# Decoder trunk on one core: hh and hl level with the weights modulo 512 bytes, a norm's rows loaded later, another order of the conformer's output chunks

## Chip, core and metric

One core of a Trainium2 chip runs the whole program. The metric is the device time of one execution in microseconds; the number quoted for a kernel is the median of its runs.

## What is computed

Two layers on x of shape (1, 256, 1024) in float32. Layer 0 mixes with causal block attention and a Mamba-2 scan side by side, layer 1 with a conformer convolution module. Behind every mixer and every feed-forward stands a norm of the residual sum:

```python
for layer in range(2):
    mixed = moba_ssd_mixer(x, ...) if layer == 0 else conformer_conv_module(x, ...)
    x = layer_norm(DN_ALPHA * x + mixed, ln_mix_g[layer], ln_mix_b[layer])
    x = layer_norm(DN_ALPHA * x + swiglu_ffn(x, ...), ln_ffn_g[layer], ln_ffn_b[layer])

def swiglu_ffn(x, w_gate, w_up, w_down):          # 1024 -> 2816 -> 1024
    return (silu(x @ w_gate) * (x @ w_up)) @ w_down

def conformer_conv_module(x, ...):
    val, gate = split(x @ w_pw1 + b_pw1)
    h = causal_depthwise_conv(val * sigmoid(gate), dw_w, dw_b)   # width 31
    return silu(layer_norm(h)) @ w_pw2 + b_pw2
```

## The kernel before

**Weights.** All weights come as 94 chunks of 1 MB, 128 partitions x 2048 numbers, in the order in which they are used. `Flow` streams them: SyncE loads a chunk into wr (three buffers, L445), ScalarE copies each half of it rounded to float32r into wh (L464), and VectorE writes the rest wr - wh into wl (L465). wh and wl have five buffers each. A chunk's place in that ring comes free with `flow.free()`, behind its last matmul.

**Matmuls.** A product of float32 numbers is made of three float32r matmuls: high by high, low by high, high by low (`mm3`, L538 to L540). x itself lies transposed in xhl, high and low parts side by side, so that a gate or up projection needs two matmuls for each block (`wstat2`): the stationary wh against 512 columns of xhl (L715), and wl against the 256 high ones (L716). The result h of a feed-forward's column block j is split into hh and hl (L821, L822). `xstat_out` takes the down projection for two blocks at a time: 24 matmuls with hh or hl stationary and 512 columns of weights moving. The program's names for the outputs are f (gate and up), fh (the first blocks, `by_halves`), fa (down), op (the mixer's output projection, with mh and ml stationary), p (the conformer's), end (the last quarter of the second feed-forward, 256 wide).

**A norm** (`boundary`) works in token halves t and column halves f. `tail(t, f)` does the last chunks' matmuls into one quarter, `sum` adds the residual and takes statistics, `center` and `fin` finish, `flip` transposes x for the next stage. The rows of gain and offset lie in gb, one buffer of 1 MB, broadcast over the partitions by `ln_rows`; the load waits until the norm before has read the buffer. The conformer's output projection has four chunks, the mixer's and the feed-forwards' tails have two.

**The conformer's taps** (`taps`): part of the depthwise convolution runs on TensorE as small matmuls pc against hs, shifted copies that come back through DRAM (hd, then hs), before a transpose ct. The bias of the output projection is put into its four PSUM banks by one matmul each (L1383).

**Order.** The code records all instructions. `issue_order` then simulates the engines with modelled costs and writes an order for each engine: at each step the ready instruction with the longest tail of work behind it, within a patience, SyncE's loads not over 400 matmuls ahead. Within an engine (SyncE's queue too) instructions run in that order, and one that waits holds all behind it.

**Places in SBUF.** Pools lie one behind the other, so an unused tile at the start of one moves all behind it. Where tiles begin in a partition of the built programs, in bytes modulo 512:

| tiles | before | after |
|---|---|---|
| xhl (x, in pool cp) | 128 | 128 |
| wr, wh, wl (pool wp) | 288 | 224 |
| mh, ml of the mixer | 288 | 224 |
| hh, hl of the first feed-forward | 416 | 224 |
| hh, hl of the second | 352 | 224 |

All slices that the matmuls take begin a multiple of 512 bytes further on.

Of the kernel before, what the change touches and what calls it, by code (L numbers as in the profile page):

```python
# [10 lines left out]
F32 = mybir.dt.float32  # L11
# [6 lines left out]
P = 128  # L18
# [4 lines left out]
NJ = HID // P  # L23
# [69 lines left out]
def issue_order(tc, nc, pools):  # L93
# [6 lines left out]
    ins = [i for i in trace if str(i.opcode) not in fixed]  # L100
# [64 lines left out]
    eng = [i.engine for i in ins]  # L165
# [94 lines left out]
    for k in range(N):  # L260
        for j in deps[k]:
            succ[j].append(k)
    dur = [max(c, d * 4 / 360.0) if eng[k] == SP else c for k, (c, d) in enumerate(zip(cst, dma_n))]

# [244 lines left out]
def trunk(ctx: ExitStack, tc: tile.TileContext, pools, w, prm, rows, x, xw, out):  # L509
# [4 lines left out]

    ctx.enter_context(pools.pool(name="gap0", bufs=1)).tile([P, 24], F32, name="gap0")
    wp = ctx.enter_context(pools.pool(name="wp", bufs=1))
    ctx.enter_context(pools.pool(name="gap1", bufs=1)).tile([P, 8], F32, name="gap1")
    pacc = ctx.enter_context(pools.pool(name="pacc", bufs=4, space=PSUM))
# [111 lines left out]
    def boundary(n, tail, acc, gb, head):  # L630
# [10 lines left out]
        for f in range(2):  # L641
            nm.center(0, f)
        tail(1, 0)
        for f in range(2):
            nm.fin(0, f, head is None)
        if head is None:
# [21 lines left out]
            return  # L668
        tail(1, 1, range(tail.n - 1))
        lo0 = nm.flip(0, 0)  # L670
# [114 lines left out]
    class Ffn:  # L785
# [37 lines left out]

        def run(self, last=False):

            nd = NJ // 2
            acc = None
            for j in range(NX, NJ):
                o = wstat2(f"f{self.n}_{j}")
                flow.add(self.side(j, o))  # L830
                if j % 2 == 1 and j < NJ - 1:
                    d = (j - 3) // 2
                    if acc is None:
                        acc = acc4(f"fa{self.n}")
                    xstat_out(acc, [self.h[2 * d + i] for i in range(2)], d == 0,
                              last and j == NJ - 3)
# [3 lines left out]
                                     for d in (nd - 2, nd - 1)])  # L840
            return acc, tail

# [394 lines left out]
    def to_ffn0():  # L1237
# [3 lines left out]
        dg["p"] = dgp.tile([P, 4 * sum(QUADS)], F32, name="dp")  # L1241
        return scope("f0")

    def scope(name):
        st = ExitStack()
        return st, st.enter_context(pools.pool(name=name, bufs=1))

# [17 lines left out]
    flow.add(diagonals(), 70)  # L1265
    gb = ln_rows(1)
    acc, tail = f0.run()

# [181 lines left out]
    def to_ffn1():  # L1450
        cv.st.close()
        return scope("f1")

    f1 = Ffn(1)
    boundary(2, tail, acc, gb, lambda m: f1.head(to_ffn1(), m))
    gb = ln_rows(3)
    acc, tail = f1.run(True)
    boundary(3, tail, acc, gb, None)
# [108 lines left out]
```

## Time and profile before

| | |
|---|---|
| median of 3 runs | 611.28 us (610.76 to 611.39) |
| the profiled execution | 612.4 us |
| its span, first to last instruction | 610.7 us |
| granted TensorE clock, mean of the span | 0.997 of full speed |
| busy: TensorE, VectorE, ScalarE, GpSimd | 595.2, 429.8, 348.0, 63.3 us |
| moved by DMA | 112.37 MB, mean 184 GB/s |

The times are of one profiled execution. PE is TensorE's matmuls, PEld its loads of stationary operands, DVE is VectorE, ACT ScalarE, POOL GpSimd, SPq the DMA issues of SyncE. In a timeline the first number is the start, the second the duration in us; matmuls that follow each other overlap, so the distance of their starts is the pace. Names carry no buffer numbers in the profile.

### The profile page before, as it was taken

What the parts mean: (1) busy time and instruction counts of PE and PEld (TensorE: products, weight loads), DVE (VectorE), ACT (ScalarE), POOL (GpSimd) and SP (SyncE); (2) the same over time, 40 slices, a digit from 0 to 9 for tenths busy, and PEclk for the clock granted to TensorE, in tenths of its full rate; (3) what the DMA queues carried; (4) which work ended last, traced back from release to release, by engine and by line L of the source; (5) the groups of instructions that cost most, each with busy time, mean ns of one, the idle gap of its engine ahead of it and who ended that gap; (6) DMA issues with size and microseconds to landing.
All of it is one profiled execution on the core that took longest, in us unless ns stands there. A gap on an engine that the chain in (4) does not pass through costs nothing.

```text
span 610.7 us, 9423 instructions
## 1 busy us (share of the span) xinstructions
PE 595.2 (97%) x3662; PEld 506.1 (83%) x3662; DVE 429.8 (70%) x723; ACT 348.0 (57%) x613; POOL 63.3 (10%) x98
## 2 busy tenths in 40 slices
PE   8999999999999999999999999899899999999995
PEld 7989898778888888888879885787788888888884
DVE  5788876698596556656697897889756556655636
ACT  5867977447455545554647862565645545555521
POOL 2100020000260000000013941200000000000002
PEclk9999999999999999999999999999999999999998
DMA  8857345428445645555516954726855554554101
GB/s 286 313 242 276 138 151 195 139 77 333 165 188 208 205 162 187 204 175 175 202 70 235 232 152 94 273 86 231 320 203 197 208 190 165 196 201 165 49 0 70
DMA packets 22497, 112.37 MB, mean 184 GB/s; under 512 B 2866, under 2 KB 8242, under 8 KB 10164
## 3 DMA queue, kind: packets, MB, share of 16 engines
q1 hardware_dynamic: 22452, 111.77, 52.3%
q8 instruction: 29, 0.48, 0.3%
q14 instruction: 16, 0.13, 0.1%
HBM read 109.59 MB, written 2.17 MB: 183 GB/s over the span
## 4 chain that ended last, share of the span: by engine, by line
PE 84%; DVE 6%; DMA 3%; ACT 3%; issue 1%; POOL 1%; SPq 0%; DVEq 0%; ACTq 0%; POOLq 0%
PE f L715 23%; PE f L716 12%; PE fa L538 6%; PE fa L540 6%; PE fa L539 6%; PE fh L738 3%; DVE wl L465 2%; PE pc L1356 2%; DMA wr<-in_w_dram 1%; PE op L540 1%; PE p L539 1%; PE p L540 1%; PE p L538 1%; PE op L538 1%; PE op L539 1%
## 5 line engine op out<-in xcount | busy, mean ns | idle before, releaser
L465 DVE TENSOR_TENSOR wl<-wr,wh 128x1024 fp32r<-128x1024 f32 (+1 forms) x188 | 228.5, 1232 | 51.5 <-ACT wh L464 49.0
L464 ACT ACTIVATE wh<-wr 128x1024 fp32r<-128x1024 f32 (+1 forms) x188 | 191.7, 1045 | 78.3 <-issue 43.4
L715 PE MATMUL f<-xhl,wh 128*128 128x512 f32 x640 | 225.4, 394 | 1.5 <-DVE hl L809 1.5
L716 PE MATMUL f<-xhl,wl 128*128 128x256 f32 x640 | 178.5, 279 | 0.0
L715 PEld LDWEIGHTS f<-xhl,wh 128*128 128x128 f32 x640 | 120.0, 187 | 30.4 <-DVE hl L809 1.9
L716 PEld LDWEIGHTS f<-xhl,wl 128*128 128x128 f32 x640 | 120.0, 188 | 1.0
L538 PE MATMUL fa<-wh,hh 128*128 128x512 f32 x172 | 68.0, 395 | 0.0
L539 PE MATMUL fa<-wl,hh 128*128 128x512 f32 x172 | 67.8, 394 | 0.0
L540 PE MATMUL fa<-wh,hl 128*128 128x512 f32 x172 | 67.8, 395 | 0.0
L816 DVE TENSOR_TENSOR h<-f,h 128x256 f32<-128x256 f32 x40 | 17.0, 424 | 70.6 <-ACT h L815 70.6
L573 POOL TENSOR_TENSOR rd<-rs,mhalf 128x1 f32<-128x1 f32 x8 | 4.4, 548 | 377.6 <-DVE rs L570 377.6
L815 ACT ACTIVATE h<-f 128x256 f32<-128x256 f32 x40 | 15.4, 385 | 41.3 <-PE f L716 41.3
L540 PEld LDWEIGHTS fa<-wh,hl 128*128 128x128 f32 x172 | 32.3, 188 | 8.0 <-DVE hl L822 0.3
L538 PEld LDWEIGHTS fa<-wh,hh 128*128 128x128 f32 x172 | 32.3, 188 | 8.0 <-ACT hh L821 0.4
L539 PEld LDWEIGHTS fa<-wl,hh 128*128 128x128 f32 x172 | 32.3, 188 | 6.7
L818 ACT ACTIVATE g<-g 128x256 f32<-128x256 f32 x40 | 16.7, 418 | 34.8 <-DVE g L816 34.8
L1336 POOL TENSOR_TENSOR ap<-ap,pr 128x256 f32<-128x256 f32 x35 | 28.0, 815 | 30.3 <-ACT pr L1335 14.5
L815 ACT ACTIVATE g<-f 128x256 f32<-128x256 f32 x40 | 15.4, 386 | 22.4 <-PE f L716 21.1
L538 PE MATMUL pw<-xhl,wh 128*128 128x256 f32 x96 | 27.5, 287 | 0.0
L540 PE MATMUL pw<-xhl,wl 128*128 128x256 f32 x96 | 27.2, 283 | 0.0
L539 PE MATMUL pw<-xhl,wh 128*128 128x256 f32 x96 | 27.1, 282 | 0.0
L738 PE MATMUL fh<-wh,xhl 128*128 128x512 f32 x64 | 21.6, 405 | 0.3 <-ACT xhl L627 0.2
(267 smaller groups left out, 999.7 us busy)
## 6 DMA issues: line engine op xcount, KB each, us to landing
wr<-in_w_dram SPq DMA_DIRECT2D x92, 1024.0 KB, 4.9
gb<-in_rows_dram SPq DMA_DIRECT2D x4, 1024.0 KB, 6.3
hs<-hd SPq DMA_DIRECT2D x20, 136.0 KB, 3.9
hs<-hd SPq DMA_DIRECT2D x12, 134.0 KB, 3.4
wr<-in_w_dram SPq DMA_DIRECT2D x4, 256.0 KB, 7.1
xw<-in_xw_dram SPq DMA_DIRECT2D x2, 512.0 KB, 7.9
xtok<-in_x_dram SPq DMA_DIRECT2D x1, 1024.0 KB, 7.1
out_dram<-xtok SPq DMA_DIRECT2D x4, 256.0 KB, 2.1
```

The lines of the kernel that those rows point to most:

```text
L464: self.nc.scalar.activation(hi, src, AF.Copy)
L465: self.nc.vector.tensor_sub(lo, src, hi)
L538: pe.matmul(o, lh, rh, start=start, stop=False)
L539: pe.matmul(o, lh, rl, start=False, stop=False)
L540: pe.matmul(o, ll, rh, start=False, stop=stop)
L715: pe.matmul(o[c], hi[:, sl], xhl[:, k], start=k == 0, stop=False)
L716: pe.matmul(o[c][:, 0, :], lo[:, sl], xh[:, k, :], start=False, stop=k == KT - 1)
L738: pe.matmul(o, part[:, k, half(t)], w[:, sl], start=part is xh and w is hi and k == 0, stop=part is xl and k == KT - 1)
L815: act.activation(a, p[:, 1, :], AF.Copy)
L816: vec.tensor_add(a, p[:, 0, :], a)
L818: act.activation(g, g, AF.Silu)
L1336: pool.tensor_tensor(ap, ap, pr, ALU.add)
```

## The change

Four edits. Unused tiles of 96 and 112 numbers are put ahead of the pools f0 and f1, so that hh and hl begin at the same place modulo 512 bytes as the weights, and the first unused tile shrinks from 24 to 8 numbers, which moves the weights and all behind them by 64 bytes against x. The rows gb of the norm behind a feed-forward are asked for when its block 11 of 22 is recorded, no longer ahead of block 2. In `boundary` the chunks of the tail but the last two go through both column halves of the second token half first; only the conformer's tail has such chunks (57 and 58, of 57 to 60). And the planner takes 230 GB/s for broadcast loads and 190 for rows under 2 KB in place of 360.

```diff
@@ -260,7 +260,17 @@
     for k in range(N):
         for j in deps[k]:
             succ[j].append(k)
-    dur = [max(c, d * 4 / 360.0) if eng[k] == SP else c for k, (c, d) in enumerate(zip(cst, dma_n))]
+
+    rate = [360.0] * N
+    for k, i in enumerate(ins):
+        if eng[k] == SP:
+            ap = list(aps(i.ins)[0].ap)
+            if ap[-1][1] * 4 < 2048:
+                rate[k] = 190.0
+            elif any(s == 0 and n > 1 for s, n in ap):
+                rate[k] = 230.0
+    dur = [max(c, d * 4 / r) if eng[k] == SP else c
+           for k, (c, d, r) in enumerate(zip(cst, dma_n, rate))]
 
 
     tail = [0.0] * N
@@ -512,9 +522,12 @@
     cp = ctx.enter_context(pools.pool(name="cp", bufs=1))
 
 
-    ctx.enter_context(pools.pool(name="gap0", bufs=1)).tile([P, 24], F32, name="gap0")
+    def gap(st, n, name):
+        st.enter_context(pools.pool(name=name, bufs=1)).tile([P, n], F32, name=name)
+
+    gap(ctx, 8, "gap0")
     wp = ctx.enter_context(pools.pool(name="wp", bufs=1))
-    ctx.enter_context(pools.pool(name="gap1", bufs=1)).tile([P, 8], F32, name="gap1")
+    gap(ctx, 8, "gap1")
     pacc = ctx.enter_context(pools.pool(name="pacc", bufs=4, space=PSUM))
     pgu = ctx.enter_context(pools.pool(name="pgu", bufs=2, space=PSUM))
     pms = ctx.enter_context(pools.pool(name="pms", bufs=2, space=PSUM))
@@ -640,7 +653,11 @@
         nm.stat(0)
         for f in range(2):
             nm.center(0, f)
-        tail(1, 0)
+
+        early = range(tail.n - 2)
+        tail(1, 0, early)
+        tail(1, 1, early)
+        tail(1, 0, range(tail.n - 2, tail.n))
         for f in range(2):
             nm.fin(0, f, head is None)
         if head is None:
@@ -666,7 +683,7 @@
             for f in range(2):
                 nc.sync.dma_start(out[0, half(1), cols(f)], xtok[:, 1, cols(f)])
             return
-        tail(1, 1, range(tail.n - 1))
+        tail(1, 1, (tail.n - 2,))
         lo0 = nm.flip(0, 0)
         nm.sum(1, 0)
         tail(1, 1, (tail.n - 1,))
@@ -821,12 +838,14 @@
             act.activation(hh, h, AF.Copy)
             vec.tensor_sub(hl, h, hh)
 
-        def run(self, last=False):
+        def run(self, rows, last=False):
 
             nd = NJ // 2
             acc = None
             for j in range(NX, NJ):
                 o = wstat2(f"f{self.n}_{j}")
+                if j == NJ // 2:
+                    gb = ln_rows(rows)
                 flow.add(self.side(j, o))
                 if j % 2 == 1 and j < NJ - 1:
                     d = (j - 3) // 2
@@ -838,7 +857,7 @@
             ch = [flow.next() for _ in range(2)]
             tail = tail_of(acc, ch, [[self.h[2 * d + i] for i in range(2)]
                                      for d in (nd - 2, nd - 1)])
-            return acc, tail
+            return acc, tail, gb
 
 
     l0 = ExitStack()
@@ -1239,10 +1258,12 @@
         dgp = ctx.enter_context(pools.pool(name="dg", bufs=1))
         dg["q"] = dgp.tile([P, 4 * sum(QUADS), 32], F32, name="dq")
         dg["p"] = dgp.tile([P, 4 * sum(QUADS)], F32, name="dp")
-        return scope("f0")
-
-    def scope(name):
+        return scope("f0", 96)
+
+    def scope(name, n=0):
         st = ExitStack()
+        if n:
+            gap(st, n, "gap" + name)
         return st, st.enter_context(pools.pool(name=name, bufs=1))
 
     dw = prmt[:, C_DW:C_DW + 8 * CONF].rearrange("p (c k) -> p c k", c=8)
@@ -1263,8 +1284,7 @@
     f0 = Ffn(0)
     boundary(0, tail, acc, gb, lambda m: f0.head(to_ffn0(), m))
     flow.add(diagonals(), 70)
-    gb = ln_rows(1)
-    acc, tail = f0.run()
+    acc, tail, gb = f0.run(1)
 
 
     co = []
@@ -1449,12 +1469,11 @@
 
     def to_ffn1():
         cv.st.close()
-        return scope("f1")
+        return scope("f1", 112)
 
     f1 = Ffn(1)
     boundary(2, tail, acc, gb, lambda m: f1.head(to_ffn1(), m))
-    gb = ln_rows(3)
-    acc, tail = f1.run(True)
+    acc, tail, gb = f1.run(3, True)
     boundary(3, tail, acc, gb, None)
     f1.st.close()
```

The order, engine by engine, changes at these places. SyncE, ahead of the second feed-forward (wr is a chunk's load, gb3 the rows of the last norm). Before:

```order
L445 DMA wr63_3940<-in_w_dram 128x2048
L445 DMA wr64_4347<-in_w_dram 128x2048
L445 DMA wr65_4367<-in_w_dram 128x2048
L583 DMA gb3_4523<-in_rows_dram 128x2048
L445 DMA wr66_4432<-in_w_dram 128x2048
L445 DMA wr67_4444<-in_w_dram 128x2048
L445 DMA wr68_4509<-in_w_dram 128x2048
```

After:

```order
L455 DMA wr63_3945<-in_w_dram 128x2048
L455 DMA wr64_4338<-in_w_dram 128x2048
L455 DMA wr65_4358<-in_w_dram 128x2048
L455 DMA wr66_4380<-in_w_dram 128x2048
L455 DMA wr67_4449<-in_w_dram 128x2048
L455 DMA wr68_4506<-in_w_dram 128x2048
L596 DMA gb3_5206<-in_rows_dram 128x2048
```

gb3 stands three loads later. (Ahead of the first feed-forward gb1 moves in the same way, by two.) ScalarE, at the start of the second feed-forward (sgt is the gate of the first blocks, hh their result, g the gate of block 2). Before:

```order
L803 ACTIVATE sgt_4517<-fh110_4474 128x128
L803 ACTIVATE sgt_4520<-fh110_4474 128x128
L464 ACTIVATE wh66_4511<-wr66_4432 128x1024
L808 ACTIVATE hh1_0_4450<-ht01_4541 128x128
L808 ACTIVATE hh1_1_4455<-ht11_4545 128x128
L464 ACTIVATE wh66_4511<-wr66_4432 128x1024
L815 ACTIVATE g_4595<-f1_20_4525 128x256
```

After:

```order
L820 ACTIVATE sgt_4532<-fh110_4485 128x128
L820 ACTIVATE sgt_4535<-fh110_4485 128x128
L474 ACTIVATE wh66_4508<-wr66_4380 128x1024 x2
L825 ACTIVATE hh1_0_4461<-ht01_4550 128x128
L825 ACTIVATE hh1_1_4466<-ht11_4554 128x128
L832 ACTIVATE g_4602<-f1_20_4538 128x256
```

Both halves of chunk 66 now stand ahead of the two hh; on VectorE one half of wl66 does likewise ahead of hl. VectorE, in the norm behind the conformer (p210 and p211 are the last two quarters). Before:

```order
L465 TENSOR_TENSOR wl61_3943<-wr61_3718,wh61_3942 128x1024
L599 SCALAR_TENSOR_TENSOR p210_4223<-xtok_83,p210_4223 128x512
L465 TENSOR_TENSOR wl62_4350<-wr62_3828,wh62_4349 128x1024 x2
L600 BN_STATS st21_4204<-p210_4223 128x6
L465 TENSOR_TENSOR wl63_4370<-wr63_3940,wh63_4369 128x1024
L599 SCALAR_TENSOR_TENSOR p211_4225<-xtok_83,p211_4225 128x512
```

After:

```order
L475 TENSOR_TENSOR wl61_3948<-wr61_3723,wh61_3947 128x1024
L475 TENSOR_TENSOR wl62_4341<-wr62_3833,wh62_4340 128x1024
L612 SCALAR_TENSOR_TENSOR p210_4228<-xtok_83,p210_4228 128x512
L475 TENSOR_TENSOR wl62_4341<-wr62_3833,wh62_4340 128x1024
L613 BN_STATS st21_4209<-p210_4228 128x6
L641 TENSOR_TENSOR xhl_82<-lt200_4386,xhl_82 128x4x128
L612 SCALAR_TENSOR_TENSOR p211_4230<-xtok_83,p211_4230 128x512
```

One half of wl stands between the two sums where three stood; the first half of wl63 went behind the norm. TensorE, the end of the taps (pc5 to pc7 are the channels' taps, p200 to p211 the bias). Before:

```order
L1356 MATMUL pc5_3744<-hs5_3731,dq_1543 32x256 x15
L1356 MATMUL pc6_3857<-hs6_3841,dq_1543 32x256 x5
L1363 MATMUL ct5_4050<-ident_85,hc5_4048 128x128 x2
L1356 MATMUL pc6_3857<-hs6_3841,dq_1543 32x256 x15
L1383 MATMUL p200_4153<-bp2_3162,ones_3163 128x512
L1356 MATMUL pc7_3966<-hs7_3953,dq_1543 32x128
L1363 MATMUL ct6_4078<-ident_85,hc6_4076 128x128 x2
L1356 MATMUL pc7_3966<-hs7_3953,dq_1543 32x128 x19
```

After:

```order
L1376 MATMUL pc5_3749<-hs5_3736,dq_1543 32x256 x15
L1403 MATMUL p200_4158<-bp2_3167,ones_3168 128x512
L1376 MATMUL pc6_3862<-hs6_3846,dq_1543 32x256
L1383 MATMUL ct5_4055<-ident_85,hc5_4053 128x128 x2
L1376 MATMUL pc6_3862<-hs6_3846,dq_1543 32x256 x19
L1376 MATMUL pc7_3971<-hs7_3958,dq_1543 32x128 x20
L1403 MATMUL p201_4160<-bp2_3167,ones_3168 128x512
L1383 MATMUL ct6_4083<-ident_85,hc6_4081 128x128 x2
```

The bias matmul p200 went ahead of channel 6, channel 6's transposes ct6 behind all of channel 7's first taps.

## Rows read from the trace of the kernel before

**Rows 1.** The page: span, and busy us (share) xinstructions of each engine.

```profile
span 610.7 us, 9423 instructions
PE 595.2 (97%) x3662; PEld 506.1 (83%) x3662; DVE 429.8 (70%) x723; ACT 348.0 (57%) x613; POOL 63.3 (10%) x98
```

**Rows 2.** The page's groups: busy us, mean ns, idle before.

```profile
L715 PE MATMUL f<-xhl,wh 128*128 128x512 f32 x640 | 225.4, 394 | 1.5 <-DVE hl L809 1.5
...
L538 PE MATMUL fa<-wh,hh 128*128 128x512 f32 x172 | 68.0, 395 | 0.0
```

**Rows 3.** TensorE's timeline, first feed-forward: start us, duration us, instruction.

```profile
256.32 0.40 PE L715 MATMUL f<-xhl,wh 128*128 128x512 f32 x1
...
267.53 0.39 PE L538 MATMUL fa<-wh,hh 128*128 128x512 f32 x1
...
273.11 0.40 PE L715 MATMUL f<-xhl,wh 128*128 128x512 f32 x1
```

**Rows 4.** TensorE's timeline, second feed-forward, one run of 24.

```profile
491.01 0.40 PE L538 MATMUL fa<-wh,hh 128*128 128x512 f32 x1
...
496.61 0.39 PE L715 MATMUL f<-xhl,wh 128*128 128x512 f32 x1
```

**Rows 5.** TensorE's timeline, the mixer's output projection.

```profile
96.99 0.39 PE L538 MATMUL op<-wh,mh 128*128 128x512 f32 x1
...
99.75 0.38 PE L1113 MATMUL ps<-kk,qh 128*128 128x128 f32 x2
...
118.03 0.39 PE L538 MATMUL op<-wh,mh 128*128 128x512 f32 x1
...
123.24 0.39 PE L540 MATMUL op<-wh,ml 128*128 128x512 f32 x1
```

**Rows 6.** TensorE's timeline, start of the second feed-forward; in brackets idle before, releaser.

```profile
430.39 0.39 PE L715 MATMUL f<-xhl,wh 128*128 128x512 f32 x1
432.33 0.50 PE L715 MATMUL f<-xhl,wh 128*128 128x512 f32 x1 [1.54 <-DVE hl L809]
```

**Rows 7.** TensorE's timeline, the 256-wide matmuls at the end.

```profile
600.76 0.28 PE L539 MATMUL end<-wl,hh 128*128 128x256 f32 x1
...
602.80 0.28 PE L539 MATMUL end<-wl,hh 128*128 128x256 f32 x1
```

**Rows 8.** SyncE's timeline, 410 to 432.

```profile
420.69 0.33 SPq L583 DMA_DIRECT2D gb<-in_rows_dram  x1
422.32 6.65 SPq L445 DMA_DIRECT2D wr<-in_w_dram  x3
```

**Rows 9.** The page's DMA issues: count, KB each, median us to landing.

```profile
wr<-in_w_dram SPq DMA_DIRECT2D x92, 1024.0 KB, 4.9
```

**Rows 10.** ScalarE's timeline, 427 to 432.5.

```profile
430.72 1.06 ACT L464 ACTIVATE wh<-wr 128x1024 fp32r<-128x1024 f32 x1 [2.71 <-DMA wr<-in_w_dram]
431.69 0.43 ACT L808 ACTIVATE hh<-ht 128x128 fp32r<-128x128 f32 x2
```

**Rows 11.** TensorE's waits: us in total, times, longest us.

```profile
PE ct L1363 <- DVE hc L1360: 1.0, 3, 0.6
...
PE lt L624 <- DVE xtok L618: 0.4, 1, 0.4
PE fh L738 <- ACT xhl L627: 0.2, 1, 0.2
```

**Rows 12.** VectorE's timeline in the norm behind the conformer.

```profile
413.63 1.21 DVE L465 TENSOR_TENSOR wl<-wr,wh 128x1024 fp32r<-128x1024 f32 x1
```

**Rows 13.** TensorE's timeline, the last matmul of that norm's tail.

```profile
413.86 0.40 PE L540 MATMUL p<-wh,xhl 128*128 128x512 f32 x1
```

**Rows 14.** TensorE's timeline, the end of the conformer's taps.

```profile
378.34 1.02 PE L1356 MATMUL pc<-hs,dq 128*32 128x256 f32 x10 [1.20 <-DMA hs<-hd]
...
381.52 0.51 PE L1383 MATMUL p<-bp,ones 128*128 128x512 f32 x1
381.96 0.41 PE L1356 MATMUL pc<-hs,dq 128*32 128x128 f32 x2
```

## The prediction

> **What bounds the kernel now.** I read four views in this order. First the busy shares of the page: TensorE is busy 595.2 us of a span of 610.7 us and no other engine comes near it [rows 1]. So the time is TensorE's pace plus the few holes in it. VectorE, ScalarE and the loads matter only where TensorE waits for them. The page's groups then say where the pace is decided: 640 pairs in the two feed-forwards (a 512-wide L715, and with each a 256-wide L716) and 516 matmuls of the down projection, 172 at L538 and as many at L539 and L540 [rows 2].
>
> The group's mean of 394 ns is the time from start to result, and successive matmuls overlap. The pace is the distance between starts, so I take it from the timeline. Between 256.32 and 267.53 stand 32 pairs: 11.21 / 32 = 0.350 us a pair. From 267.53 to 273.11 stand 24 down-projection matmuls: 0.2325 us each [rows 3]. The same 24 in the second feed-forward take (496.61 - 491.01) / 24 = 0.2333 us [rows 4]. The mixer's output projection has the same shapes and the same order of operands, yet between 118.03 and 123.24 it takes 5.21 / 23 = 0.2265 us; its first run, 12 matmuls from 96.99 to 99.75, takes 0.2300 [rows 5]. What differs between them is where the stationary tile begins against the weights: level for the mixer's mh and ml, 128 bytes behind for the first feed-forward's hh and hl, 64 for the second's.
>
> Last I read TensorE's waits. The largest behind the start of the program is at 430.39: the next matmul starts at 432.33 [rows 6].
>
> **The change part by part.** *hh and hl level with the weights.* This touches the pace of 264 down-projection matmuls in the first feed-forward (11 pairs of chunks, 24 each) and of the other 252 in the second. At the mixer's settled pace they would save 264 x (232.5 - 226.5) + 252 x (233.3 - 226.5) ns = 1.6 + 1.7 = 3.3 us, which is the upper end; the lower end is 0, if the offset is not what makes the difference. A run is 24 long and follows matmuls of another kind, so I take the mixer's unsettled 230.0 for its first 12 and 226.5 for its last 12, a mean of 228.25: 264 x 4.25 + 252 x 5.05 ns = **2.4 us**. All of it lies on the path, since TensorE hardly waits in these stages.
>
> A rule speaks against this term. The Trainium skill ("TensorE: Matmul & The Clock Gate", Part 2: What happens when you issue a matmul) says that loading the next tile's weights takes no SBUF read bandwidth from the running matmul, and its page "SBUF — State Buffer" (SBUF: two separate sides) says that PE waits on no one there. By that rule offsets cannot matter and the term is 0. The 226.5 against 232.5 and 233.3 ns speak for an offset; by the rule the sum would be 2.4 us smaller.
>
> *The smaller gap ahead of the weights.* It shifts wh and wl by 64 bytes against x (xhl), so the 640 pairs, which read x against the weights, go from an offset of 160 bytes to one of 96. No row shows 96. The nearest rows are the offsets of 64 and 128, both 6 to 7 ns a matmul above the level pace [rows 3 to 5], and the pairs themselves at 160. A level 512 and the 256-wide matmuls at the end, (602.80 - 600.76) / 18 = 0.1133 us [rows 7], would make a pair of 0.2265 + 0.1133 = 0.3398; the present excess is 10.5 ns, times 640 = 6.7 us. So the bounds are 6.7 us gained (the excess goes) and 6.7 lost (it doubles). Every offset seen for 512-wide matmuls other than 0 costs about the same, so I take **0**.
>
> *The norm's rows loaded in mid feed-forward, and chunks 0 and 1 of the conformer's output through both halves first.* These meet at the norm before the second feed-forward. There SyncE issues gb at 420.69, when the norm has let go of the buffer, and only then the load of chunk 66, at 422.32 [rows 8]. The two megabytes share the queues: ScalarE gets chunk 66 at 430.72, after 2.71 us of waiting [rows 10], 8.4 us behind the issue, where such a load takes 4.9 at the median [rows 9]. Queued behind that wh on ScalarE are the two hh copies at 431.69. They and hl empty the bank that TensorE needs next, so TensorE's 1.94 us at 430.39, 1.7 of them lost, is this late load [rows 6, 10].
>
> In the changed order gb stands three loads later. The load of chunk 66 still waits until VectorE has split chunk 63, at about 422.3 as now or up to 0.5 later (one half of wl more stands behind the norm, which itself ends a little sooner), and with the median lands at 427.2 to 427.7. ScalarE is free at 428.0 (430.72 less 2.71). But now both halves of chunk 66 stand ahead of hh: 428.0 + 2 x 1.06 = 430.1, and from the first hh to TensorE's start it was 432.33 - 431.69 = 0.64, so 430.8 against the 430.6 at which TensorE wants the bank. The stall shrinks to about 0.2: **1.5 us** gained. Bounds: 1.7 gained; 1.1 lost, if the load lands as late as now and hh waits for one half more.
>
> At the first feed-forward gb moves behind two loads in the same way, but no wait of TensorE stands there: 0, hidden by the split chunks that are ahead; bounds 0 and the 0.2 us for which fh waits for ScalarE's xhl, TensorE's only wait at that norm [rows 11].
>
> The chunk order lets chunks 57 and 58 go 12 matmuls earlier, and VectorE then does one half of wl instead of three between the norm's last two sums. Now a half started at 413.63, 1.21 long, holds the second quarter's sum until 414.8 [rows 12], although its last matmul (413.86, 0.40 long) is done at 414.3 [rows 13]; the norm then keeps the flips lt waiting 0.4 us [rows 11]. I take **0.3**, bounds 0 and 0.4. The first quarter is summed 12 matmuls later; that is covered by the second quarter's matmuls. If that cover went, up to 12 x 0.233 = 2.8 us would be lost.
>
> *The planner's new DMA rates.* They change no duration, only the order. The place that counts is the end of the conformer's taps: a bias matmul that held the next taps from 381.52 to 381.96 now stands ahead of channel 6, where TensorE waits 1.20 us for hs [rows 14]. I take **0.3** of that 0.44; bounds 0.4 gained and 0.6 lost (the longest wait of the transposes ct [rows 11], if channel 6's, now behind 20 more taps, come late). The few swaps in the first 60 us move no load: 0, covered by split chunks ahead.
>
> **Sum:** 2.4 + 0 + 1.5 + 0.3 + 0.3 = 4.5 us. The profiled execution took 612.4 us, so 607.9; the median of the runs, 611.28, is 1.1 below that execution, so 606.8 us.
>
> **Rivals.**
> - *The offset of hh does nothing* (the change then doesn't do what it says). For it: the mixer's runs are few, and its first ones are no faster than 230. Against: 23 steady steps at 226.5. It gives 606.8 + 2.4 = 609.2. This is the Trainium skill's rule from above, by its two pages.
> - *The new offset of x against the weights pays.* For it: pairs stand 10.5 ns above the level pace, so there is something to win. Against: 64 and 128 won nothing for the 512-wide matmuls. Half of the excess gives 606.8 - 3.4 = 603.4, all of it 600.1.
> - *It costs a little*, 4 to 6 ns a pair: 2.6 to 3.8 us, so about 610.3.
> - *It costs a lot* (the other side). Stationary weights and moving x meet twice as often in each of the 640 pairs: 6.7 us lost, 613.5. It decides from 4.5 + 1.2 = 5.7 us, 8.9 ns a pair, a pair of 0.359 us. For it: no row shows 96. Against: three offsets all cost about one step of 6.7 ns and none two.
> - *The load of chunk 66 still lands late*: 608.3 if the stall stays as it is, 609.4 if it grows by the second half.
>
> **How the numbers follow.** A measurement of this kernel can tell about 0.2%, 1.2 us, from no change: faster is below 610.1, slower above 612.5. Chances: forecast 0.54, all faster; the new offset pays 0.14, faster; hh does nothing 0.14, of which 0.11 faster and 0.03 same; the load still late 0.05, of which 0.03 faster and 0.02 same; costs a little 0.06, same; costs a lot 0.07, slower. So 0.82 faster, 0.11 same, 0.07 slower. The range goes from 602.8 (the forecast with its terms at their upper ends, 0.9 + 0.2 + 0.1 + 0.1 us, and about 2.7 us of the offset) to 610.4 (the small cost); it leaves out the large cost, the rest of the large gain and a part of the small cost.
>
> **What would show it.** Down-projection matmuls 226 to 230 ns apart in both feed-forwards; pairs still at 0.350; no wait over 0.5 us near 430; chunk 66's load in before gb and landing within 5.5 us; the bias matmul in the hole before channel 6. I am wrong if the pairs' distance moves by more than 3 ns, or if 516 matmuls keep 232.5 and 233.3.

## The result, and the profile after

The changed kernel takes **602.84 us** (median; 602.50 to 603.14, 4 runs) against 611.34 for the kernel before in the same comparison (610.76 to 612.50, 4 runs): a ratio of 0.9858, 95% interval 0.9841 to 0.9876. That is 8.5 us faster where 4.5 was forecast, at the very end of the range of 602.8 to 610.4 (taken by the ratio from the forecast's base of 611.28 us, it is 602.6). The profiled execution took 603.14 us, its span is 601.4, 9.3 less than before's 610.7, at a granted clock of 0.998 (0.997 before).

The page of the changed kernel, span and busy shares, then its groups (busy us, mean ns), to be read against [rows 1, 2]:

```profile
span 601.4 us, 9425 instructions
PE 588.6 (98%) x3662; PEld 504.7 (84%) x3662; DVE 429.6 (71%) x723; ACT 347.8 (58%) x613; POOL 63.1 (10%) x98
...
L732 PE MATMUL f<-xhl,wh 128*128 128x512 f32 x640 | 223.2, 392 | 0.0
L733 PE MATMUL f<-xhl,wl 128*128 128x256 f32 x640 | 178.8, 280 | 0.0
...
L551 PE MATMUL fa<-wh,hh 128*128 128x512 f32 x172 | 67.3, 391 | 0.0
```

TensorE does the same 3662 matmuls in 6.6 us less busy time, and the 1.5 us that stood as idle ahead of the pairs are gone. The bound is the same; its pace and its holes changed. TensorE's timeline of the changed kernel, same places as [rows 3, 4] (start us, duration us):

```profile
254.21 0.40 PE L732 MATMUL f<-xhl,wh 128*128 128x512 f32 x1
...
265.31 0.39 PE L551 MATMUL fa<-wh,hh 128*128 128x512 f32 x1
...
270.75 0.40 PE L732 MATMUL f<-xhl,wh 128*128 128x512 f32 x1
...
483.26 0.39 PE L551 MATMUL fa<-wh,hh 128*128 128x512 f32 x1
...
488.71 0.40 PE L732 MATMUL f<-xhl,wh 128*128 128x512 f32 x1
```

The 32 pairs take 11.10 us, 0.3469 a pair (before 0.3503). The 24 down-projection matmuls take 5.44 and 5.45, 0.2267 and 0.2271 each (before 0.2325 and 0.2333). TensorE's waits (us in total, times, longest), whose counterparts are [rows 6, 11, 14]:

```profile
PE ct L1383 <- DVE hc L1380: 0.9, 3, 0.4
PE cb L1408 <- DVE zt L1395: 0.6, 1, 0.6
PE fh L755 <- ACT xhl L640: 0.5, 2, 0.2
PE lt L637 <- DVE xtok L631: 0.5, 1, 0.5
```

Two waits are missing: the 1.5 us for hl at the start of the second feed-forward, and the 1.2 us for hs ahead of channel 6. The transposes lt still wait for a norm, 0.5 us, but not for the one behind the conformer. Before the change that wait stands at 319.79, in the norm behind the first feed-forward (in the changed kernel at 317.15), and the conformer's norm let the flips go without any. (The second wait of fh for xhl, 0.25 us, is new at the conformer's norm.) TensorE's timeline of the kernel before:

```profile
319.79 0.63 PE L624 MATMUL lt<-ident,xtok 128*128 128x128 f32 x4 [0.38 <-DVE xtok L618]
...
412.27 0.60 PE L624 MATMUL lt<-ident,xtok 128*128 128x128 f32 x4
...
414.10 0.60 PE L624 MATMUL lt<-ident,xtok 128*128 128x128 f32 x4
```

The end of the taps, in TensorE's timeline (compare [rows 14]):

```profile
374.25 0.49 PE L1403 MATMUL p<-bp,ones 128*128 128x512 f32 x1
374.67 0.62 PE L1376 MATMUL pc<-hs,dq 128*32 128x256 f32 x2
375.22 0.44 PE L1383 MATMUL ct<-ident,hc 128*128 128x128 f32 x2
...
381.00 0.49 PE L1403 MATMUL p<-bp,ones 128*128 128x512 f32 x1
381.82 0.30 PE L1383 MATMUL ct<-ident,hc 128*128 128x128 f32 x1 [0.33 <-DVE hc L1380]
...
383.86 0.66 PE L1408 MATMUL cb<-ident,zt 128*128 128x128 f32 x4 [0.62 <-DVE zt L1395]
```

The bias matmul does stand ahead of channel 6, but in this execution there is no hole there for it to fill.

ScalarE's timeline at the start of the second feed-forward, then SyncE's (compare [rows 8, 10]):

```profile
422.79 2.01 ACT L474 ACTIVATE wh<-wr 128x1024 fp32r<-128x1024 f32 x2
424.69 0.44 ACT L825 ACTIVATE hh<-ht 128x128 fp32r<-128x128 f32 x2
```

```profile
417.20 0.33 SPq L455 DMA_DIRECT2D wr<-in_w_dram  x1
...
423.91 0.43 SPq L596 DMA_DIRECT2D gb<-in_rows_dram  x1
```

Chunk 66 is asked for at 417.20, its rounding starts at 422.79 with no wait for a load, and gb comes 6.7 us later.

Where the 9.3 us between the two profiled executions come from, in sums of the distances from one matmul's start to the next (the stall is 1.94 less the 0.24 that such a step takes without it):

| place | before | after | gained |
|---|---|---|---|
| 516 down-projection matmuls fa | 120.37 | 117.61 | 2.76 |
| 640 pairs, stall at 430 taken out | 224.46 | 222.29 | 2.17 |
| stall at 430 | 1.70 | 0 | 1.70 |
| channel 5's first tap to the first cb | 15.12 | 12.82 | 2.30 |
| all else, by difference | | | 0.4 |

### The profile page after: what moved, and what is told of

Read it like the earlier page. It is cut to its first block, busy times and chain, and to the rows that moved or that the text cites. A ratio compares the mean times of both kernels' runs of the same rounds, so it can differ in the third digit from the quotient of the medians.

```text
span 601.4 us, 9425 instructions
## 1 busy us (share of the span) xinstructions
PE 588.6 (98%) x3662; PEld 504.7 (84%) x3662; DVE 429.6 (71%) x723; ACT 347.8 (58%) x613; POOL 63.1 (10%) x98
## 3 DMA queue, kind: packets, MB, share of 16 engines
HBM read 109.59 MB, written 2.17 MB: 186 GB/s over the span
## 4 chain that ended last, share of the span: by engine, by line
PE 85%; DVE 6%; ACT 4%; POOL 2%; issue 1%; DMA 1%; SPq 0%; DVEq 0%; POOLq 0%; ACTq 0%
PE f L732 24%; PE f L733 12%; PE fa L551 6%; PE fa L553 6%; PE fa L552 6%; PE fh L755 4%; PE pc L1376 2%; DVE wl L475 2%; ACT wh L474 2%; POOL ap L1356 1%; PE op L553 1%; PE p L553 1%; PE p L552 1%; PE op L551 1%; PE p L551 1%; PE op L552 1%
```

## The experiments

My theory after the result: the pace of a matmul goes by where its stationary tile lies against its moving one, for hh and for x; the stall at 430 was the late load of chunk 66; and the conformer's part is only in part the planner's order. The rival: the new order on ScalarE, VectorE and the queues made everything faster, and the places nothing. Each edit can be made alone, and the places can be moved without touching the order of any engine.

**hh and hl level, nothing else.** The order on every engine is that of before.

```diff
-        return scope("f0")
+        return scope("f0", 96)
...
-        return scope("f1")
+        return scope("f1", 112)
```

> The kernel before with one edit, the unused tiles ahead of the pools f0 and f1: hh and hl begin level with the weights, everything else at its old place and in its old order. Theory (a matmul's pace goes by where the stationary tile begins against the moving one, modulo 512 bytes): down-projection matmuls at 227 ns in both feed-forwards in place of 232.5 and 233.3, pairs still at 0.350 us, the 1.94 us at 430 and the hole ahead of channel 6 still there; 516 x 5.5 ns = 2.8 us gained, about 608.5. Rival (the offset does nothing, the shorter distances of the changed kernel come from its other order on ScalarE, VectorE and the queues): 232.5 and 233.3 stay, 611.3.

Measured: 609.00 us (608.45 to 609.52, 5 runs), ratio 0.9960 (0.9946 to 0.9974). TensorE's timeline of this kernel:

```profile
255.31 0.40 PE L715 MATMUL f<-xhl,wh 128*128 128x512 f32 x1
...
266.52 0.40 PE L538 MATMUL fa<-wh,hh 128*128 128x512 f32 x1
...
272.00 0.40 PE L715 MATMUL f<-xhl,wh 128*128 128x512 f32 x1
...
429.79 0.50 PE L715 MATMUL f<-xhl,wh 128*128 128x512 f32 x1 [1.71 <-DVE hl L809]
```

Pairs 11.21 / 32 = 0.3503 us as before, down projection 5.48 / 24 = 0.2283 in place of 0.2325, all 516 of them 118.13 us in place of 120.37: 2.24 us gained, and 2.4 by the medians. The stall at 430 is there. What I had wrong in this expectation is the hole ahead of channel 6: it is gone, though no engine's order changed.

By the Trainium skill's rule ("TensorE: Matmul & The Clock Gate", Part 2: What happens when you issue a matmul), that the next tile's weight load takes no read bandwidth from the running matmul, the place of hh could make no difference. Here the same instructions in the same order stand 228 or 232.5 ns apart by the place of the pool of hh, and the measurement decides; that it is read bandwidth which they lose is not shown. The edit moves the other tiles of that pool too. The kernels further down in which hh stays and the weights' place changes give the same: only level is fast.

**The weights 64 bytes lower, nothing else.** Again the order of before on every engine; hh and hl move along and keep their offsets of 128 and 64.

```diff
-    ctx.enter_context(pools.pool(name="gap0", bufs=1)).tile([P, 24], F32, name="gap0")
+    ctx.enter_context(pools.pool(name="gap0", bufs=1)).tile([P, 8], F32, name="gap0")
```

> The kernel before with one edit, the first unused tile of 8 numbers in place of 24: weights and all behind them 64 bytes lower, so the offset of x against the weights is 96 in place of 160, while hh and hl keep their offsets of 128 and 64. Theory: pairs at 0.347 us, 640 x 3.4 ns = 2.2 us, and some 0.6 us from the mixer's 256-wide matmuls, which also read x against weights: about 608.5; down-projection still at 232.5 and 233.3. Rival (the other order, not the place, made the pairs faster): pairs at 0.350 and 611.3. My prediction's value for this edit was 0.

Measured: 608.24 us (607.77 to 609.14, 5 runs), ratio 0.9950 (0.9936 to 0.9964). TensorE's timeline:

```profile
255.10 0.39 PE L715 MATMUL f<-xhl,wh 128*128 128x512 f32 x1
...
266.21 0.39 PE L538 MATMUL fa<-wh,hh 128*128 128x512 f32 x1
...
271.79 0.39 PE L715 MATMUL f<-xhl,wh 128*128 128x512 f32 x1
```

Pairs 11.11 / 32 = 0.3472, down projection unchanged at 0.2325. The place of x against the weights is worth 3.1 us by the medians; the step that my prediction set to 0 was by the medians the largest single edit (95% interval 2.2 to 3.9 us). Of the 3.4 us between the two spans 1.9 are the pairs and 0.4 the mixer's 256-wide matmuls between 34 and 97 us, which read x against the weights too; 0.9 more are a shorter hole ahead of channel 6, which is not the edit's doing, as the end of this part shows.

**The changed kernel with the weights back up.** The order is that of the changed kernel.

```diff
-    gap(ctx, 8, "gap0")
+    gap(ctx, 24, "gap0")
```

> The changed kernel with the first unused tile back at 24 numbers, its order untouched: offset of x against the weights 160 again, hh and hl still level. Theory: pairs back at 0.350, 2.2 to 2.8 us lost, 605.0 to 605.6; down-projection stays at 227. Rival (the order made the pairs faster): 602.8. Second question: does the hole ahead of channel 6 stay away; if it comes back with the place, the conformer's gain is not the order's.

Measured: 606.58 us (605.87 to 608.91, 6 runs), ratio 0.9926 (0.9910 to 0.9943): 3.7 us slower than the changed kernel, somewhat more than I expected. Pairs are back at 0.3503; the down projection, though still level, costs 0.5 us more in all (118.15 against 117.61): the first eight distances of a run scatter between 225 and 236 ns and settle at 227 from there on (means over 18 runs), as with hh level alone, where those of the changed kernel stand at 227 from the second. What the pairs are like is felt in the run behind them. The hole ahead of channel 6 stays away.

**x level with the weights too.**

```diff
-    gap(ctx, 8, "gap0")
+    gap(ctx, 112, "gap0")
```

> The changed kernel with 112 numbers in the first unused tile, its order untouched: x level with the weights too (all at 128 modulo 512), hh and hl still level. Theory in its simple form (level is best for every matmul): pairs at 0.3398, 640 x 7 ns = 4.5 us more gained, near 598. Theory in a second form (the end's 256-wide matmuls went from 113 to 120 ns when they became level, so 256-wide ones lose a step of 6.7 ns where 512-wide ones win one): pairs at 0.227 + 0.120 = 0.347, no gain there, about 602.8, and the mixer's 256-wide ones at 120: about 0.6 us lost, 603.4. Rival (the place modulo 512 of each tile by itself matters, not the difference): no rule for it, down-projection matmuls leave 227.

Measured: 606.85 us (606.59 to 607.06, 5 runs), ratio 0.9924 (0.9910 to 0.9939): 4.0 us slower than the changed kernel. Neither form of the theory had this. TensorE's timeline:

```profile
255.58 0.39 PE L732 MATMUL f<-xhl,wh 128*128 128x512 f32 x1
...
266.87 0.40 PE L551 MATMUL fa<-wh,hh 128*128 128x512 f32 x1
...
272.37 0.39 PE L732 MATMUL f<-xhl,wh 128*128 128x512 f32 x1
```

A pair takes 11.29 / 32 = 0.3528, the longest so far: the 512-wide matmul rose from 230 to 236 ns and the 256-wide one stayed at 117 (medians). Yet plain runs of 512-wide matmuls that read weights against x, fh and pwh among them, fell to 227 ns when level (232 in the changed kernel). So "level is best" holds for runs of equal 512-wide matmuls, not for pairs of a 512 and a 256.

**The rows of a norm in mid feed-forward, alone.** TensorE's order is that of before.

```diff
                 o = wstat2(f"f{self.n}_{j}")
+                if j == NJ // 2:
+                    gb = ln_rows(rows)
...
```

> The kernel before with one edit: a norm's rows asked for at block 11 of the feed-forward. TensorE's order is that of before; gb3 stands three loads later, both halves of chunk 66 ahead of hh on ScalarE. Theory: the load of chunk 66 lands within 5.5 us of its issue and the 1.94 us at 430 shrink to 0.24 (1.7 us gained), about 609.7. Rival (the chunk order of the norm before is what freed the start of the second feed-forward): 1.9 us still there, or longer by one half of wh more ahead of hh, 611.3 to 612.4. Second question: does the hole ahead of channel 6, 1.6 us in the profile of before, stand here too, where nothing at the conformer is changed? If it differs, it comes and goes between executions.

Measured: 609.44 us (608.35 to 609.64, 7 runs), ratio 0.9961 (0.9947 to 0.9975). The 1.5 us wait for hl is gone from the waits, and the distances there gain 1.75 us: the theory. The hole ahead of channel 6 is gone too, where nothing was changed.

**The chunk order, alone.**

```diff
-        tail(1, 0)
+        early = range(tail.n - 2)
+        tail(1, 0, early)
+        tail(1, 1, early)
+        tail(1, 0, range(tail.n - 2, tail.n))
...
-        tail(1, 1, range(tail.n - 1))
+        tail(1, 1, (tail.n - 2,))
```

> The kernel before with one edit: chunks 57 and 58 go through both halves of the output projection first. Theory: nothing at the norm (the flips wait 0.4 us as before), and the 1.94 us at 430 stay, because gb3 still stands ahead of chunk 66's load and now both halves of wh stand ahead of hh: 611.3 to 612.4. My prediction's value: 0.3 us gained. Rival (this edit freed the start of the second feed-forward): 1.7 us gained, 609.6.

Measured: 611.66 us (609.73 to 614.03, 12 runs), ratio 1.0004 (0.9989 to 1.0019). TensorE's waits:

```profile
PE f L718 <- DVE hl L812: 1.8, 1, 1.8
PE pc L1359 <- DMA hs<-hd: 1.3, 1, 1.3
...
PE lt L624 <- DVE xtok L618: 0.4, 1, 0.4
```

The flips' wait of 0.4 us is the one in the norm behind the first feed-forward; at the norm that this edit touches there was none to win, and the edit earns nothing. The stall is 0.3 us longer, because the second half of chunk 66 now stands ahead of hh as well.

The profiled execution, the slowest of the twelve, shows that the stall can cost more than its own length. Behind the 1.8 us in which TensorE did nothing, up to 432.3, its granted clock fell to 0.50, the lower of its two levels (1.2 GHz in place of 2.4), from about 433.5 to 437. Two of these microseconds (length, busy time and count of PE, PEld, DVE, ACT and POOL, then clock and DMA):

```profile
434.00:436.00 2.00, 2.00 (x9) 1.71 (x8) 2.00 (x2) 1.02 (x2) 0.00 (x0) 0.50 0.75 176
```

From the first pair of the second feed-forward to its last quarter this execution takes 1.8 us longer than the profiled one of before, where the clock stayed at 1.00 behind the same stall: 0.25 are the longer stall, the rest the clock. The three executions of this kernel with a mean granted clock of 0.993 took 613.2 to 614.0 us, the nine others (0.996 to 0.998) 609.7 to 612.2.

**The planner's rates, alone.**

```diff
-    dur = [max(c, d * 4 / 360.0) if eng[k] == SP else c for k, (c, d) in enumerate(zip(cst, dma_n))]
+            if ap[-1][1] * 4 < 2048:
+                rate[k] = 190.0
+            elif any(s == 0 and n > 1 for s, n in ap):
+                rate[k] = 230.0
+    dur = [max(c, d * 4 / r) if eng[k] == SP else c
+           for k, (c, d, r) in enumerate(zip(cst, dma_n, rate))]
```

> The kernel before with one edit: the planner's rates for broadcast and narrow loads. Theory: the end of the conformer's taps gains 0.5 to 0.8 us beyond the hole ahead of channel 6 (the kernels with this order gained 2.1 to 2.4 us there, those with the old order 1.0 to 1.5, and 1.6 of it is the hole that the profile of before shows): 610.5 to 610.9; no hole there; pairs and down-projection as before; 1.9 us at 430 as before. Rival (the order is worth the whole 2.35 us): 609.0. My prediction's value: 0.3 us.

Measured: 608.78 us (608.21 to 609.26, 6 runs), ratio 0.9953 (0.9939 to 0.9968), below the rival's value, and for a reason that neither had: the stall at 430 is gone here as well. ScalarE's timeline:

```profile
427.81 0.51 ACT L817 ACTIVATE hh<-ht 128x128 fp32r<-128x128 f32 x2 [1.30 <-PE ht L816]
429.15 1.06 ACT L473 ACTIVATE wh<-wr 128x1024 fp32r<-128x1024 f32 x1 [0.82 <-DMA wr<-in_w_dram]
```

gb is still ahead of chunk 66, and that load still comes late (issued at 420.73, used at 429.15, 8.4 us as before). But the planner, counting more time for gb, expects it late and puts hh ahead of the waiting half. So two of the edits remove the same stall, one by an earlier load, one by the order on the waiting engine.

**Every fifth place of the ring at another offset.** Since pairs follow neither "offset does not matter" nor "level is best", I read the rule off one kernel: unused tiles between the places of the ring of weights give each its own offset to x, while every engine's order stays that of the changed kernel. The next two kernels are the same with other numbers.

```diff
-        self.parts.append(
-            (self.pool.tile([P, 2048], F32R, name=f"wh{i}", tag="wh", bufs=RING),
-             self.pool.tile([P, 2048], F32R, name=f"wl{i}", tag="wl", bufs=RING)))
+        b = i % RING
+        if i < RING and PADS[b]:
+            self.pool.tile([P, PADS[b]], F32, name=f"pad{b}", tag=f"pad{b}", bufs=1)
+        self.parts.append(
+            (self.pool.tile([P, 2048], F32R, name=f"wh{i}", tag=f"wh{b}", bufs=1),
+             self.pool.tile([P, 2048], F32R, name=f"wl{i}", tag=f"wl{b}", bufs=1)))
```

> The changed kernel, its order untouched, with unused tiles between the five places of the ring of weights, so that they begin 64, 96, 128, 192 and 224 bytes behind x modulo 512 in turn (hh and hl as far from them as that makes it). One look: the pace of the pairs, place by place. Theory (the difference of places sets the pace): the place at 96 shows 0.347 us a pair as in the changed kernel; those at 64 and 128 between 0.347 and 0.351; if one lies below 0.345, there is a better place for the weights, worth 640 ns a ns. Rival (the place by itself, or the neighbours in SBUF): the place at 96 is not at 0.347, or all five alike.

> As the scan of 64 to 224, with the five places of the ring 256, 320, 384, 448 and 480 bytes behind x modulo 512. What the first scan showed, pairs of 347.0 at 96 and 347.2 at 224 against 351 to 352.6 at 64, 128 and 192, and 352.9 at 0, speaks for minima 128 bytes apart. Theory A (only the difference modulo 128 counts): 480 near 347, 256, 320, 384 and 448 at 351 to 353. Theory B (the whole difference modulo 512 counts): no such pattern; some place may come nearer to 340, the distance of a level 512-wide and an undisturbed 256-wide matmul.

> As the other two scans, with the places 288, 352, 416, 448 and 0 bytes behind x modulo 512; 448 and 0 are there a second time, as controls. Theory A: 352 near 347, 288 and 416 at 350 to 351 (as 160 was, 350.6), 448 and 0 at 351 to 353. Theory B: no such pattern. If neither 0 gives 353 nor 448 what it gave in the other scan, the pace is not set by the difference of places alone.

Measured, one run each: 607.59, 607.65 and 607.82 us (hh and hl are mostly not level in them). The mean distance of the pairs by place, 117 to 120 pairs each:

| place behind x, bytes | pair, ns |
|---|---|
| 96, 224, 480; 352 | 347.0, 347.2, 347.3; 346.9 |
| 288, 416 (and 160 in the kernel before) | 353.0, 350.1 (350.6) |
| 64, 192, 320; 448 in both | 352.6, 351.1, 351.8; 351.6 and 350.6 |
| 128, 256, 384; 0 (and 0 in the level kernel) | 351.0, 349.8, 350.5; 352.4 (352.9) |

In TensorE's timeline of the last of the three, blocks 14 (place 352), 16 (place 0), 17 (place 288) and the down projection behind it:

```profile
239.25 0.39 PE L738 MATMUL f<-xhl,wh 128*128 128x512 f32 x1
...
244.80 0.39 PE L738 MATMUL f<-xhl,wh 128*128 128x512 f32 x1
...
256.01 0.39 PE L738 MATMUL f<-xhl,wh 128*128 128x512 f32 x1
...
261.65 0.39 PE L738 MATMUL f<-xhl,wh 128*128 128x512 f32 x1
...
267.31 0.39 PE L557 MATMUL fa<-wh,hh 128*128 128x512 f32 x1
...
272.90 0.39 PE L738 MATMUL f<-xhl,wh 128*128 128x512 f32 x1
```

Sixteen pairs take 5.55 us at place 352, 5.64 at 0 and 5.66 at 288. The control at 96 gives the changed kernel's own 347, and 0 and 448 repeat within 1 ns. The pattern is theory A's: the four places that are 96 modulo 128 stand together at 347, and the eleven others lie between 349.8 and 353.0 (288 above the 350 to 351 that theory A gave it; 32 was not tried). No place comes near 340. These are means, and what ran before a block counts too: at 256 the blocks right behind a down projection take 346.6 a pair and those behind other pairs 353.3, and 192 and 448 hold the first block of each feed-forward, at 355.8 to 358.5, while their other blocks take 348.7 to 351.9. At the four good places every block lies between 346.7 and 347.8.

x itself began at 128 in every kernel. For the pairs, therefore, the offset against x and the weights' own place modulo 512 are not told apart; the rival that their own place counts stands. For the down projection it falls: runs of 24 were level with the tiles at 96, 128, 224, 288 and 352 (worked out from the unused tiles) and took 5.44 to 5.50 us each time. With hh 32, 64, 96, 128, 160 or 224 bytes off the weights they take 5.59 to 5.62 (267.31 to 272.90 is 160 off), against 5.47 or 5.48 for the level ones in the same three kernels. So there only level pays, and 96, the best for pairs, does not.

**The changed kernel with the planner's old rates.**

```diff
...
-    dur = [max(c, d * 4 / r) if eng[k] == SP else c
-           for k, (c, d, r) in enumerate(zip(cst, dma_n, rate))]
+    dur = [max(c, d * 4 / 360.0) if eng[k] == SP else c for k, (c, d) in enumerate(zip(cst, dma_n))]
```

> The changed kernel with the planner's old rate of 360 for all loads. Theory (the new order is worth 0.7 us at the end of the conformer's taps, and it keeps away a hole of up to 1.6 us there, which kernels with the old order show in some executions and not in others; the later gb3 alone keeps the stall at 430 away): 0.7 us slower than the changed kernel in an execution without the hole, 2.3 with it, so 603.5 to 605.2, with a wider spread of its runs. No wait over 0.5 us near 430. Rival (the planner's rates decide nothing): 602.8. Rival (the rates were needed at 430 too): 604.5 without the hole, with 1.7 us at 430.

Measured: 603.62 us (603.27 to 605.79, 5 runs), ratio 0.9871 (0.9850 to 0.9893); 0.8 us slower than the changed kernel by the medians, which the intervals of the two ratios do not tell from no difference; the trace shows 0.74 of it at the taps. There is no stall near 430 and no hole in the profiled execution. That is the theory's lower case.

**Places and rates only.**

```diff
...
-    acc, tail, gb = f1.run(3, True)
+    gb = ln_rows(3)
+    acc, tail = f1.run(True)
...
-        early = range(tail.n - 2)
-        tail(1, 0, early)
-        tail(1, 1, early)
-        tail(1, 0, range(tail.n - 2, tail.n))
+        tail(1, 0)
```

> The changed kernel without two of its edits: gb asked for where it was, chunks 57 and 58 in the old order; the places of the tiles and the planner's rates as changed. Theory (rates alone already put hh ahead of chunk 66 on ScalarE and so remove the stall at 430, and the chunk order is worth nothing): the same as the changed kernel, 602.5 to 603.2. Rival (the later gb and the chunk order are worth something of their own, as my prediction had it with 0.3): 603.3 to 604.6.

Measured: 603.13 us (602.40 to 604.93, 5 runs), ratio 0.9855 (0.9835 to 0.9876), the changed kernel's ratio. Its profiled execution lost 1.9 us against the changed kernel's in the first 20 us, where the first matmuls waited 2.0 us in one piece for rounded weights (1.0 in two pieces there) and then ran at a granted clock of 0.50 between 12 and 14 us; from there to the end it kept that distance within 0.2 us. With the new rates, the later gb and the chunk order earn nothing that shows. The three edits that remain add up: 2.4 (hh level) + 3.1 (x) + 2.7 (rates) = 8.2 us by their own medians, of 8.8 for the three together. No kernel tried beats the changed one by more than the measurement can tell.

**The end of the conformer's taps, over all kernels.** From channel 5's first tap to the first cb, one profiled execution each:

| order there | kernel: us (wait for hs ahead of channel 6) |
|---|---|
| old | before 15.12 (1.2); chunk order 15.18 (1.3); weights lower 14.19 (0.3); hh level 13.56, gb later 13.57, changed with old rates 13.56 (none) |
| new | changed 12.82; rates 12.84; weights back up 12.98; x level 12.83; places and rates 12.83; two of the scans 12.82, 12.81 (none); scan of 256 to 480 13.08 (0.2) |

Each channel has four copies hs, so of the last eight that SyncE issues the first four are channel 6's and the last four channel 7's. SyncE's timeline of before, and then with hh level:

```profile
371.67 4.67 SPq L1327 DMA_DIRECT2D hs<-hd  x8
```

```profile
370.45 3.62 SPq L1329 DMA_DIRECT2D hs<-hd  x8
```

The fourth of these issues alone, the last number its us from issue to landing, in before and then with hh level:

```profile
hs<-hd SPq DMA_DIRECT2D x1, 136.0 KB, 5.2
```

```profile
hs<-hd SPq DMA_DIRECT2D x1, 136.0 KB, 3.3
```

The hole ends with channel 6's fourth copy. In before it lands at 378.14 and TensorE goes on at 378.34 [rows 14], 0.20 us later; with the chunk order it is 377.87 and 378.07, with the weights lower 375.62 and 375.82. The eight issues take longer in before because one of them took 1.48 us in place of 0.43, but that is the eighth, of channel 7, which lands at 379.59, when TensorE has long gone on. It goes along with slow copies: in six of the fourteen profiled executions one of the last two issues took 1.15 to 1.83 us and the fourth copy 4.25 to 5.25 us, in the eight others no issue took over 0.44 and that copy took 3.07 to 3.46. What held them is not shown. Three of the six have the old order (before, chunk order, weights lower) and three the new (weights back up, two scans), so no edit sorts them; with one trace for each kernel, how often it happens is not known.

So the profile of before carried up to 1.6 us that a run need not have. Where the copies are early, the new order is worth 0.74. Where they are late it is worth more, and then the bias matmul ahead of channel 6 does fill the hole. In the weights-back-up kernel and two scans the fourth copy lands 3.5 to 3.8 us behind channel 5's first tap. The old order wants it at 3.3 and goes on 0.2 behind the landing, which would make holes of 0.4 to 0.8 us (an estimate from these numbers); the three lost 0 to 0.3.

## Why the prediction was right in direction and wrong in size

- **hh and hl level: right.** 2.4 us forecast, 2.24 in the trace and 2.4 by the medians alone, 2.76 together with the new place of x. The mechanism holds too: with hh level alone the first third of a run is unsettled and the rest stands at 227 ns, a mean of 228.3 where I took 228.25. The rival "the offset of hh does nothing" fell.
- **The smaller gap ahead of the weights: the step that failed.** I took 0 because "every offset seen for 512-wide matmuls other than 0 costs about the same". Those offsets were seen in runs of equal matmuls, and pairs follow another rule: 96 modulo 128 is 3.4 ns better than 160, and level is worse than either. Measured: 3.1 us alone, 3.7 on top of the rest. The rival "the new offset of x against the weights pays" is what happened, at a third of the excess in the pairs (2.2 of 6.7 us), with 0.4 in the mixer and 0.5 in the down projection beside it. My bound of 6.7 us, a pair of level matmuls at 339.8 ns, was no bound that any place reached. Its 113.3 ns for a 256-wide matmul stand in that one execution alone: with hh at the same offset of 64 the same matmuls stood 117.8 ns apart in four other kernels. The test I had set, a pair's distance moving by more than 3 ns, is met: 3.4.
- **gb three loads later: right.** 1.5 forecast, 1.7 measured, with chunk 66 issued 5.1 us earlier as all else there, landing within 5.6 us, and gb behind it, as written. What I did not see is that the planner's rates remove the same stall by themselves.
- **The norm's sums: 0.3 forecast, 0 measured; a wait read at the wrong place.** I charged the 0.4 us of [rows 11], a total that names no place, to the norm behind the conformer. It stands at 319.79, in the norm behind the first feed-forward, which this edit does not touch. One half of wl stood between the sums as the order said, but TensorE waited for no flip there, so there was nothing to win.
- **The planner's rates: 0.3 forecast, 0.74 measured, by another hole.** I put the gain into the wait ahead of channel 6, which is there only in executions with late copies. In the changed kernel's execution there was none, and the gain stands at the end: a bias matmul that stood ahead of channel 7's last 40 taps now stands behind them, the last transpose waits 0.33 in place of 0.56, and cb waits 0.62 for zt in place of 1.02; these two make 0.63 of the 0.74. That the order of the bias makes them shorter is read from the rows, not tried by itself.
- **Together:** of the 4.0 us missing by the medians, about 3.1 to 3.7 are the place of x and 0.4 the rates. Against the profiled execution 0.8 more are gone, which fits a hole that the medians of before hold in part; how often it stands there, one trace for each kernel cannot tell.

## What to carry to other kernels

Where TensorE is the bound, the place of the stationary tile against the moving one is a term of its own, and a rule for it found in one sequence of matmuls does not carry to another: here 512-wide runs were fastest at 0, pairs of 512 and 256 at 96 modulo 128 behind x, so measure each sequence. A ring whose places lie at different offsets measures five at once, without touching the order. And before a gain is put into a wait that one trace shows, compare it with the trace of another kernel in which that place is unchanged: the largest wait in the conformer came from copies that were late in six of fourteen executions. And a total of waits does not say where they stand: find the wait in the timeline before it is given a price.

## What the runs showed of the hardware that was not expected

- Pairs of a 512-wide and a 256-wide matmul went from 346.9 to 353.0 ns in the mean by the place of the stationary tiles alone (x stayed where it was), best at four offsets from x that lie 128 bytes apart (96, 224, 352, 480). At 0 they are slower than at most (352.4 and 352.9), where runs of 24 512-wide matmuls are fastest (5.44 to 5.50 us against 5.58 to 5.62).
- The 24 matmuls of 256 columns at the end gained nothing from being level: 119.7 ns apart in all six level kernels, against 117.8 in four kernels with an offset of 64 and 113.3 in the profile of before, with the same offset [rows 7]. What made that one execution faster is not shown.
- The same copy on SyncE's queue, 136 KB, landed 3.1 to 3.5 us behind its issue in eight executions and 4.2 to 5.3 in six, and TensorE waited up to 1.3 us for it.
- Behind the stall at 430 TensorE's granted clock fell to 0.50, the lower of its two levels, for some 3.4 us in the profiled execution of the chunk order, and stayed at 1.00 in those of before, of hh level and of the weights lower, which have the stall too.
